# A squared-ReLU MLP by seven products: the fifth and the sixth product of a block trade places

## The chip, the core and the metric

The program runs on one core of one Trainium2 chip. The metric is the device time of one execution, in microseconds (us). Times of an instruction are given in us from the start of the profiled execution's span, or in ns where marked. In the profile PE is the matrix engine (PEld its weight loads), DVE the vector engine, ACT the scalar engine, POOL the GpSimd engine and SP the engine that issues most DMAs.

## The reference

A decoder trunk of two layers on a sequence of 1024 rows and a width of 1024, in float32. Layer 0 mixes tokens with a gated convolution, layer 1 with an attention that has forget gates; each layer then attends to 256 memory tokens and ends in an MLP. The change is in the MLP, which both layers have:

```
def sqrelu_mlp(h, w1, w2):
    return jnp.square(jax.nn.relu(h @ w1)) @ w2        # w1 1024 x 4096, w2 4096 x 1024

h = rmsnorm(x, norm_ff_g[l])
x = x + sqrelu_mlp(h, ff_w1[l], ff_w2[l])
```

## The kernel before

Activations are kept transposed, as 16 tiles of 128 x 512 (`X`, eight chunks of features by two halves of the sequence). Every number that enters a matmul is split into a high part (a rounded float32, made by ACT) and a low part (the rest, made by DVE), and each product of two blocks takes three passes: low by high, high by low, high by high.

**Seven products.** A product of 2 x 2 blocks is made by seven block products instead of eight (Winograd's form). `mlp` writes it as a list, `steps`. One step is one block product for one group `g` of output columns: 4 chunks by 3 passes, 12 matmuls of 128 x 128 by 128 x 512, all into one bank of PSUM. The seven are named after their activation operand, `a11`, `a12`, `a22` (blocks) and `s1` to `s4` (sums of blocks); `WEIGHT` names the partner, and `SUM` tells which of three PSUM sums of the group a product is added to: sum 0 takes `a11`, `a12`; sum 1 takes `s2`, `s3`, `a22`; sum 2 takes `s1`, `s4`. Groups go in pairs, so that a block of the list is 14 steps: the seven products, each for `g` and then for `g + 1`. A pair has six banks (`banks(6)`), and the next pair takes them over in the same order.

**What is read between products.** A sum is read out more than once, because a partial sum is a result too: after `s2` and before `s3` is added, after `s3` and before `a22`, after `s1` and before `s4`, after `a11` and before `a12`. The matmuls of a product therefore wait until the engine that reads the partial sum of its bank has done so: ACT for `a11` (line 805 in the first half, line 955 in the second), DVE for the others (lines 812 and 814 in the first half, 967 and 971 in the second).

**Two halves.** In the first half (h @ w1, groups 0 to 15) the readouts go to `rows`, then `squares` (relu and square, ACT), and the pieces are stored to HBM: `a11` and `a12` split into high and low (`high_inner` on ACT into `uh`, `low_inner` on DVE into `ul`, four tiles in rotation), the sums `s1` to `s4` made of them by POOL (`inner_sums`) and stored by `store_rest`. In the second half (times w2, groups 16 to 31, four groups for each quarter `f` of the inner columns) `load_inner` brings these back, `high_of_inner` and `low_of_inner` split them, and `add_rows` adds the readouts to `X`. For quarter 0 `add_rows` writes into tiles of `X` that had held pieces of the first half, so it also waits for their stores. Groups 0 and 1 are made by eight plain products. The list of the pair 14, 15 (the last of the first half) is ordered by `SEVEN_TURN`, all others by `SEVEN`.

**What sets the order.** Under `in_order` each engine runs its instructions exactly as written. For every step n, `urgent[n]` (the readouts), then `before[n]` (loads, splits, sums) are emitted, then the high part of the weight of step n + 5 and the low part of that of step n + 4, then the 12 matmuls, then `after[n]`. So the readout of a step stands on DVE ahead of a weight's low part that is needed four steps later. DMAs are issued by SP in the same order. With `b` the first step of a block, the code gives positions as `b + 11`; this text counts positions 0 to 13 inside a block.

```
for n in range(len(steps) + 1):
    for f in chain(urgent[n], before[n]):
        f()
    for m, done, f in ((n + AHEAD + 1, highs, fetch_high), (n + AHEAD, fetched, fetch_low)):
        ...
```

Of the kernel before, what the change touches and what calls it, by code (L numbers as in the profile page):

```python
# [41 lines left out]

SEVEN = ("a11", "a12", "s2", "s1", "s4", "s3", "a22")

SEVEN_TURN = ("a11", "a12", "s2", "s3", "s1", "a22", "s4")

ENDING_FIRST = ("a11", "a12", "s2", "s1")
WEIGHT = {"a11": "b11", "a12": "b21", "s2": "t2", "s3": "t3", "s1": "t1", "a22": "t4", "s4": "b22"}  # L50
# [36 lines left out]
def trunk(ctx, tc, a, out):  # L87
# [512 lines left out]
    def mlp(layer, firsts_r, seconds, copy=None, ending=None):  # L600
# [5 lines left out]
        UP = FF // 256  # L606

        ud = {
            x: dram.tile([P, 2, UP, HALF] if x in SPLIT_FIRST else [P, UP, HALF], F32, name=f"u{x}{layer}")
            for x in SEVEN  # L610
        }
# [5 lines left out]
        with (  # L617
# [56 lines left out]
            base = {}  # L674
            for g in range(2, 2 * UP, 2):
                base[g] = len(steps)
                for x in SEVEN if g + 2 != UP else SEVEN_TURN:
                    steps += [(g + i, WEIGHT[x], x, (g + i, SUM[x]), pm) for i in range(2)]
            end = base[2 * UP - 2] + 14
            fetches = [n for n in range(len(steps)) if n not in again]  # L680
# [2 lines left out]
            def at(n, f, *args):  # L683
                before[n].append(partial(f, *args))

            def at_once(n, f, *args):
                urgent[n].append(partial(f, *args))

            def at_end(n, f, *args):
                after[n].append(partial(f, *args))  # L690
# [77 lines left out]
            for g, b in base.items():  # L768
                late = g == UP
# [80 lines left out]
            def split_inner_at(n, g, x):  # L850
                at(n, high_inner, g, x)
                at(n + 1, low_inner, g, x)
# [43 lines left out]
            for g, b in base.items():  # L896
                if g >= UP:
                    continue
                last = g + 2 == UP
                for i in range(2):  # L900
                    for n in range(b + i, b + 14, 2):
                        at_once(n + 1, rows, n)
                        at_end(n + 1, squares, n)
                    if g > 2:
                        split_inner_at(b + 5 + i, g + i, "a11")
                    split_inner_at(b + (14 if last else 11) + i, g + i, "a12")
                    if not last:
                        at(b + 15 + i, inner_sums, g + i, NEW, pool)
                        at(b + 17 + 2 * i, store_rest, g + i)
                    else:  # L910
                        at(b + 13 + i, inner_sums, g + i, NEW[:2], dve)
                        at(b + 15 + i, inner_sums, g + i, NEW[2:], dve)
                        at(b + 16 + i, store_rest, g + i)
# [61 lines left out]
            for f in range(4):  # L975
                lb = base[UP + 4 * f - 2]
                for k, x in enumerate(SEVEN if f else SEVEN_TURN):
                    at(lb + 2 * k + 2, load_inner, f, x)
                late = f == 0
                for x, ns in (  # L980
                    ("s2", (10, 12) if late else (8, 10)), ("s1", (14, 15) if late else (12, 13)), ("s4", (17, 18) if late else (16, 17)),
                    ("s3", (20, 21) if late else (19, 20)), ("a22", (22, 23)),
                ):
                    for j, n in enumerate(ns):
                        at(lb + n, high_of_inner, f, x, j)
                        at(lb + n + 1, low_of_inner, f, x, j)
            b = base[UP]
            for n in range(b, len(steps)):
                g, x = steps[n][0], steps[n][2]
                if x == "a11":  # L990
                    at_once(n + 1, copy_first, g % 4, n)
                    if g >= UP + 4:
                        at(n + 1, add_first, g % 4)
                else:

                    at_once(n + (4 if x in ("a12", "s2") and g < UP + 2 else 1), add_rows, n)
            for i in range(2 * NCH):
                at(b + 30 + 3 * i, load_back, i // 2, i % 2)
                at(b + 32 + 3 * i, add_back, i // 2, i % 2)
# [19 lines left out]
            b = end - 14  # L1019
# [17 lines left out]
            with in_order():  # L1037
# [17 lines left out]
                for n in range(len(steps) + 1):  # L1055
# [5 lines left out]
                    if n < len(steps):  # L1061
                        g, _, x, key, p = steps[n]
# [356 lines left out]
    xd = dram.tile([P, NCH, S], F32, name="xd")  # L1419
    first_normalized, first_weights = [], []  # L1420
    firsts, seconds = mlp(0, *sums, copy=xd, ending=lambda rb: start_fox(rb, first_normalized, first_weights))
    fox_layer(xd, first_normalized, first_weights, seconds)
    firsts, seconds = mlp(1, *mem_attention(1))
    for sl in HALVES:
        rb = firsts if sl.start == 0 else spread(rms_of_sums(seconds, RMS_EPS))
# [73 lines left out]
```

## Time and profile before

| | |
|---|---|
| time, median of 3 runs | 2811.76 us (2811.71 to 2813.89) |
| the profiled execution: its time, its span | 2810.81 us, 2809.0 us |
| PE busy | 2725.0 us, 97% of the span |
| DVE, ACT, POOL busy | 71%, 45%, 26% of the span |
| MLP of layer 0, first to last of its products | 714.8 to 1343.3 us |
| MLP of layer 1 | 2158.0 to 2792.9 us |
| granted clock of PE, mean | 0.993 |

A row of the profile's groups reads: line of the kernel, engine, operation, what it writes and reads, shapes, count | busy us, mean ns of one | idle time of that engine just before such instructions, and who ended most of it. A row of the timeline reads: start, length, engine, line, operation, count, and in brackets the idle time before it and what ended that. PE's matmuls overlap, so that the length of a row and not the mean of one matmul tells the pace.

### The profile page before, as it was taken

To read this page: it belongs to the slowest core of one execution; us is meant where nothing else is said; L and a number is where in the kernel's file an instruction comes from. 1 tells how busy PE (TensorE), PEld (TensorE's weight loads), DVE (VectorE), ACT (ScalarE), POOL (GpSimd) and SP (SyncE) were. 2 spreads that over 40 slices of the span, in tenths; PEclk is the share of its full clock that TensorE was granted. 3 is DMA by queue.
4 is the path that set the end of the run, shared out by engine and by line. 5 is a ranking of instruction groups with operands and counts; after the bars stand their busy time and mean duration, and the time that the engine had idled before them with its cause. 6 is when DMAs were issued, how large, how long until landed. Compare 5 with 4: busy or idle time off the path is not lost. (4 is left out here: it accounts for less than half of the span.)

```text
span 2809.0 us, 35852 instructions
## 1 busy us (share of the span) xinstructions
PE 2725.0 (97%) x12832; PEld 2247.6 (80%) x12832; DVE 1991.7 (71%) x3119; ACT 1275.7 (45%) x2295; POOL 720.2 (26%) x487
## 2 busy tenths in 40 slices
PE   7999999999999999999899999989999999999998
PEld 6777777888888877888688888878888788878886
DVE  5999984555776577777777777775546855677776
ACT  5112143433465563334466666663424655543332
POOL 0000000000076625784000000000000365625763
PEclk9999999999999999999899999999999999999999
DMA  6334364321265585652123222244213455565651
GB/s 220 120 120 135 110 213 124 102 91 56 80 220 181 188 303 195 214 199 91 61 87 94 89 88 77 86 143 138 96 67 105 144 183 191 203 228 194 228 203 60
DMA packets 172275, 402.26 MB, mean 143 GB/s; under 512 B 18352, under 2 KB 47408, under 8 KB 171840
## 3 DMA queue, kind: packets, MB, share of 16 engines
q1 hardware_dynamic: 171840, 399.90, 42.1%
q8 instruction: 101, 1.65, 0.2%
q14 instruction: 78, 0.64, 0.1%
q10 hardware_dynamic: 256, 0.07, 0.0%
HBM read 278.66 MB, written 117.05 MB: 141 GB/s over the span
## 5 line engine op out<-in xcount | busy, mean ns | idle before, releaser
L1070 PE MATMUL mm<-op,w 128*128 128x512 f32 x5424 | 1239.6, 390 | 20.8 <-DVE x L967 8.9
L1070 PEld LDWEIGHTS mm<-op,w 128*128 128x128 f32 x5424 | 1018.5, 188 | 238.7 <-issue 8.9
L269 PE MATMUL mm<-op,wh 128*128 128x512 f32 x1056 | 331.3, 395 | 4.7 <-DVE op L148 4.7
L148 DVE TENSOR_TENSOR w<-r,w 128x512 fp32r<-128x512 f32 x264 | 262.5, 998 | 30.2 <-ACT w L653 30.2
L653 ACT CAST w<-r 128x512 fp32r<-128x512 f32 x264 | 163.4, 623 | 259.9 <-PE mm L1070 235.2
L269 PEld LDWEIGHTS mm<-op,wh 128*128 128x128 f32 x1056 | 200.3, 190 | 50.1 <-DVE op L148 7.9
L1316 PE MATMUL mm<-op,wh 128*128 128x512 f32 x736 | 231.4, 395 | 0.0
L148 DVE TENSOR_TENSOR w<-t,w 128x512 fp32r<-128x512 f32 x180 | 176.6, 995 | 62.3 <-ACT w L653 62.0
L269 PE MATMUL mm<-op,wl 128*128 128x512 f32 x528 | 211.2, 401 | 9.4 <-DVE wl L148 6.2
L647 POOL TENSOR_TENSOR t<-r,t 128x512 f32<-128x512 f32 x104 | 174.1, 1674 | 94.4 <-DVE w L148 63.8
L207 POOL TENSOR_TENSOR r<-v,mhalf 128x4 f32<-128x4 f32 (+1 forms) x15 | 16.8, 1117 | 680.3 <-DVE v L205 680.3
L653 ACT CAST w<-t 128x512 fp32r<-128x512 f32 x180 | 111.9, 622 | 170.6 <-PE mm L1070 140.5
L865 POOL TENSOR_TENSOR x<-x,x 128x512 f32<-128x512 f32 x112 | 160.0, 1453 | 112.5 <-ACT x L878 101.6
L151 ACT CAST wh<-raw 128x1024 fp32r<-128x1024 f32 x96 | 100.6, 1049 | 190.1 <-PE mm L269 102.2
L151 ACT CAST pth<-mm 128x512 fp32r<-128x512 f32 (+1 forms) x224 | 105.9, 496 | 153.5 <-PE mm L556 80.9
L967 DVE TENSOR_TENSOR x<-mm,x 128x512 f32<-128x512 f32 x160 | 109.4, 684 | 93.1 <-PE mm L1070 75.9
L1316 PEld LDWEIGHTS mm<-op,wh 128*128 128x128 f32 x736 | 139.3, 189 | 26.9
L269 PE MATMUL mm<-op,xsh 128*128 128x512 f32 x512 | 158.0, 393 | 0.0
L1316 PE MATMUL mm<-op,wl 128*128 128x512 f32 x368 | 155.5, 423 | 2.4 <-ACT q L1336 2.4
L408 DVE SCALAR_TENSOR_TENSOR x<-d,par,x 128x512 f32<-128x512 f32 x232 | 154.5, 743 | 0.0
L647 POOL TENSOR_TENSOR t<-r,r 128x512 f32<-128x512 f32 x52 | 80.3, 1544 | 288.1 <-DMA r<-in_ff_w 239.2
L148 DVE TENSOR_TENSOR wl<-raw,wh 128x1024 fp32r<-128x1024 f32 x96 | 116.7, 1221 | 37.9 <-ACT wh L151 37.3
(187 smaller groups left out, 4569.2 us busy)
## 6 DMA issues: line engine op xcount, KB each, us to landing
r<-in_ff_w SPq DMA_DIRECT2D x128, 512.0 KB, 3.9
op<-ua SPq DMA_DIRECT2D x80, 512.0 KB, 6.8
us<-x SPq DMA_DIRECT2D x128, 256.0 KB, 2.9
op<-us SPq DMA_DIRECT2D x64, 512.0 KB, 5.3
raw<-mvo SPq DMA_DIRECT2D x32, 512.0 KB, 3.3
ua<-ul SPq DMA_DIRECT2D x64, 256.0 KB, 2.2
ua<-uh SPq DMA_DIRECT2D x60, 256.0 KB, 2.3
raw<-in_pw SPq DMA_DIRECT2D x24, 512.0 KB, 4.6
```

Of the source, the lines that this page charges most:

```text
L148: dve.tensor_tensor(lo, src, hi.bitcast(F32), op=ALU.subtract)
L151: act.copy(hi, src)
L207: pool.tensor_tensor(r, v, mhalf[:, :nb], op=ALU.pow)
L269: pe.matmul(out_ps, x, y, start=i == 0, stop=i == len(terms) - 1)
L408: dve.scalar_tensor_tensor(out[s], d[:, j : j + n], w, y, op0=ALU.mult, op1=ALU.add)
L647: (dve if g in (2, 3, UP, UP + 1) else pool).tensor_tensor(t, raws[g, x], raws[g, y], op=ALU.subtract)
L653: act.copy(highs[n][0], raws[steps[n][:2]])
L865: eng.tensor_tensor(u[g, x], y1, y2, op=op_)
L967: dve.tensor_tensor(v, sums[key], v, op=ALU.add)
L1070: pe.matmul(sums[key], y, z, start=first and i == 0, stop=n == last_of[key] and i == len(terms) - 1, skip_group_check=True,)
L1316: pe.matmul(t, x, y, start=n == 0, stop=n == len(terms) - 1)
```

## The change

The list `SEVEN` gets `s3` ahead of `s4`. It holds for the pairs 2 to 12 of the first half and 16 to 28 of the second. The pair 14, 15 keeps `SEVEN_TURN`, and the last pair, 30, keeps the old order under a new name, `SEVEN_LAST`. Four things follow the swap: the split of `a12` goes from positions 11 and 12 to 13 and 14, because its last piece is added by `s4`; the loads of the second half's operands for quarters 1 to 3 (`for k, x in enumerate(SEVEN ...)`) and the splits of `s3` and `s4` trade their slots; and in quarter 0's first pair the readout of `s2` stands one step earlier, since `s3` now follows it after two steps of `s1`.

```
-SEVEN = ("a11", "a12", "s2", "s1", "s4", "s3", "a22")
+SEVEN = ("a11", "a12", "s2", "s1", "s3", "s4", "a22")
 SEVEN_TURN = ("a11", "a12", "s2", "s3", "s1", "a22", "s4")
+SEVEN_LAST = ("a11", "a12", "s2", "s1", "s4", "s3", "a22")
...
-                for x in SEVEN if g + 2 != UP else SEVEN_TURN:
+                for x in {UP - 2: SEVEN_TURN, UP: SEVEN, 2 * UP - 2: SEVEN_LAST}.get(g, SEVEN):
...
-                    split_inner_at(b + (14 if last else 11) + i, g + i, "a12")
+                    split_inner_at(b + (14 if last else 13) + i, g + i, "a12")
...
-                    ("s2", (10, 12) if late else (8, 10)), ("s1", (14, 15) if late else (12, 13)), ("s4", (17, 18) if late else (16, 17)),
-                    ("s3", (20, 21) if late else (19, 20)), ("a22", (22, 23)),
+                    ("s2", (10, 12) if late else (8, 10)), ("s1", (14, 15) if late else (12, 13)), ("s3", (17, 18) if late else (16, 17)),
+                    ("s4", (20, 21) if late else (19, 20)), ("a22", (22, 23)),
...
-                    at_once(n + (4 if x in ("a12", "s2") and g < UP + 2 else 1), add_rows, n)
+                    at_once(n + (({"a12": 4, "s2": 3}.get(x, 1)) if g < UP + 2 else 1), add_rows, n)
```

The order on PE at positions 8 to 11 of pair 16, 17 in the MLP of layer 1. The number behind `mm_` is the bank's name: 20577 and 20594 are sum 1 of groups 16 and 17, 20612 and 20632 (20633 in the changed kernel) are sum 2. Before:

```order
L1070 MATMUL mm_20612<-op_20468,w_20557 128x512 x6
L1070 MATMUL mm_20612<-op_20469,w_20557 128x512 x6
L1070 MATMUL mm_20632<-op_20468,w_20574 128x512 x6
L1070 MATMUL mm_20632<-op_20469,w_20574 128x512 x6
L1070 MATMUL mm_20577<-op_20325,w_20591 128x512 x6
L1070 MATMUL mm_20577<-op_20326,w_20591 128x512 x6
L1070 MATMUL mm_20594<-op_20325,w_20609 128x512 x6
L1070 MATMUL mm_20594<-op_20326,w_20609 128x512 x6
```

And in the changed kernel:

```order
L1071 MATMUL mm_20577<-op_20325,w_20557 128x512 x6
L1071 MATMUL mm_20577<-op_20326,w_20557 128x512 x6
L1071 MATMUL mm_20594<-op_20325,w_20574 128x512 x6
L1071 MATMUL mm_20594<-op_20326,w_20574 128x512 x6
L1071 MATMUL mm_20612<-op_20468,w_20591 128x512 x6
L1071 MATMUL mm_20612<-op_20469,w_20591 128x512 x6
L1071 MATMUL mm_20633<-op_20468,w_20609 128x512 x6
L1071 MATMUL mm_20633<-op_20469,w_20609 128x512 x6
```

`s3` (sum 1, operands 20325 and 20326) moved ahead of `s4` (sum 2, operands 20468 and 20469); `a22` follows into 20577 and 20594 in both. Between two products into one bank stand three steps instead of one, except for `a11` and `a12`.

The order on DVE at the same place, from the readouts of `s2` and `s1` on (line 971 and, in the changed kernel, 972; lines 967 and 968 are the later readouts, 148 and 149 the low parts of operands `op` and weights `w`). Before:

```order
L971 TENSOR_TENSOR x41_15721<-mm_20612,m_20491 128x512
L148 TENSOR_TENSOR op_20325<-op_20325 128x1024
L148 TENSOR_TENSOR w_20609<-r11_17856,w_20609 128x512
L971 TENSOR_TENSOR x40_15720<-mm_20577,m_20491 128x512
L971 TENSOR_TENSOR x51_15723<-mm_20632,m_20523 128x512
L148 TENSOR_TENSOR op_20326<-op_20326 128x1024
L148 TENSOR_TENSOR w_20629<-t_20462,w_20629 128x512
L971 TENSOR_TENSOR x50_15722<-mm_20594,m_20523 128x512
L967 TENSOR_TENSOR x40_15720<-mm_20612,x40_15720 128x512
L148 TENSOR_TENSOR op_20413<-op_20413 128x1024
L148 TENSOR_TENSOR w_20650<-t_20494,w_20650 128x512
L967 TENSOR_TENSOR x50_15722<-mm_20632,x50_15722 128x512
```

And in the changed kernel:

```order
L972 TENSOR_TENSOR x40_15720<-mm_20577,m_20491 128x512
L972 TENSOR_TENSOR x41_15721<-mm_20612,m_20491 128x512
L149 TENSOR_TENSOR op_20468<-op_20468 128x1024
L149 TENSOR_TENSOR w_20609<-r11_17856,w_20609 128x512
L972 TENSOR_TENSOR x50_15722<-mm_20594,m_20523 128x512
L972 TENSOR_TENSOR x51_15723<-mm_20633,m_20523 128x512
L149 TENSOR_TENSOR op_20469<-op_20469 128x1024
L149 TENSOR_TENSOR w_20630<-t_20462,w_20630 128x512
L968 TENSOR_TENSOR x41_15721<-mm_20577,x41_15721 128x512
L149 TENSOR_TENSOR op_20413<-op_20413 128x1024
L149 TENSOR_TENSOR w_20651<-t_20494,w_20651 128x512
L968 TENSOR_TENSOR x51_15723<-mm_20594,x51_15723 128x512
```

The readout of `s2` (20577 and 20594 into `x40` and `x50`) moved up by one step, and the readouts of `s3` took the place of those of `s4`. The number and the kinds of instructions are the same.

The order on ACT where pair 2, 3 of layer 1 ends and pair 4, 5 begins (lines 796 and 797, in the changed kernel 797 and 798, are relu and square; 839 or 840 is the high part of `a12`; 805 or 806 the readout of `a11`; 653 or 654 the high part of a weight). Before:

```order
L839 CAST uh_18549<-x70_15726 128x512
L653 CAST w_18552<-r00_17853 128x512
L796 ACTIVATE x20_15716<-x20_15716 128x512
L797 ACTIVATE x20_15716<-x20_15716 128x512
L839 CAST uh_18573<-x00_15712 128x512
L653 CAST w_18576<-r10_17855 128x512
L796 ACTIVATE x60_15724<-x60_15724 128x512
L797 ACTIVATE x60_15724<-x60_15724 128x512
L653 CAST w_18599<-t_18522 128x512
L796 ACTIVATE x10_15714<-x10_15714 128x512
L797 ACTIVATE x10_15714<-x10_15714 128x512
L653 CAST w_18619<-t_18526 128x512
```

And in the changed kernel, up to the readout of `a11`:

```order
L840 CAST uh_18587<-x70_15726 128x512
L654 CAST w_18590<-t_18522 128x512
L797 ACTIVATE x10_15714<-x10_15714 128x512
L798 ACTIVATE x10_15714<-x10_15714 128x512
L840 CAST uh_18613<-x00_15712 128x512
L654 CAST w_18616<-t_18526 128x512
L797 ACTIVATE x21_15717<-x21_15717 128x512
L798 ACTIVATE x21_15717<-x21_15717 128x512
L806 COPY x01_15713<-mm_18619 128x512
```

The two casts of `a12` moved down by two steps and now stand between the squares of `a22` and right ahead of the readout of the next pair's `a11`.

## The prediction, made before the changed kernel ran

> **What bounds the kernel now.** I read the page's busy shares, then its groups of matmuls, then PE's timeline through both MLPs.
>
> ```profile
> PE 2725.0 (97%) x12832; PEld 2247.6 (80%) x12832; DVE 1991.7 (71%) x3119; ACT 1275.7 (45%) x2295; POOL 720.2 (26%) x487
> L1070 PE MATMUL mm<-op,w 128*128 128x512 f32 x5424 | 1239.6, 390 | 20.8 <-DVE x L967 8.9
> ```
>
> PE is the bound, and the matmuls of the two MLPs (line 1070) fill 1239.6 us of it. The idle time ahead of them is 20.8 us in all, so an order of these products can give back little more than that. The timeline shows each wait with its place: a row is an unbroken run of matmuls, with the idle time ahead of it in brackets. Layer 0, then layer 1:
>
> ```profile
> 793.53 239.65 PE L1070 MATMUL mm<-op,w 128*128 128x512 f32 x1056 [0.39 <-DVE x L814]
> 1036.40 27.54 PE L1070 MATMUL mm<-op,w 128*128 128x512 f32 x120 [3.22 <-ACT m L955]
> 1066.14 65.55 PE L1070 MATMUL mm<-op,w 128*128 128x512 f32 x288 [2.20 <-DVE x L967]
> 1131.89 11.21 PE L1070 MATMUL mm<-op,w 128*128 128x512 f32 x48 [0.20 <-DVE x L967]
> 1143.72 65.53 PE L1070 MATMUL mm<-op,w 128*128 128x512 f32 x288 [0.62 <-DVE x L967]
> 1209.76 11.17 PE L1070 MATMUL mm<-op,w 128*128 128x512 f32 x48 [0.51 <-DVE x L967]
> 1221.25 111.82 PE L1070 MATMUL mm<-op,w 128*128 128x512 f32 x492 [0.32 <-DVE x L967]
> ```
>
> ```profile
> 2165.33 71.00 PE L1070 MATMUL mm<-op,w 128*128 128x512 f32 x312
> 2239.49 241.28 PE L1070 MATMUL mm<-op,w 128*128 128x512 f32 x1056 [3.16 <-DVE x L814]
> 2483.09 27.51 PE L1070 MATMUL mm<-op,w 128*128 128x512 f32 x120 [2.33 <-ACT m L955]
> 2513.18 77.94 PE L1070 MATMUL mm<-op,w 128*128 128x512 f32 x336 [2.58 <-DVE x L967]
> 2592.13 65.55 PE L1070 MATMUL mm<-op,w 128*128 128x512 f32 x288 [1.01 <-DVE x L967]
> 2658.32 11.19 PE L1070 MATMUL mm<-op,w 128*128 128x512 f32 x48 [0.64 <-DVE x L967]
> 2669.81 76.57 PE L1070 MATMUL mm<-op,w 128*128 128x512 f32 x336 [0.31 <-DVE x L967]
> 2746.94 35.64 PE L1070 MATMUL mm<-op,w 128*128 128x512 f32 x156 [0.55 <-DVE x L967]
> ```
>
> Twelve matmuls are a step, so the counts give each wait its position in the list. The twelve waits for a DVE readout (lines 814 and 967) all stand at position 8, ahead of `s4`, or at position 12, ahead of `a22`: the runs of 48 matmuls, four steps, go from the one to the other. Both are products that follow, with only one step between, a product into their own bank. The two waits for ACT (line 955) stand at position 2 of pair 16, where `a12` follows `a11` at the same distance; the change leaves that distance as it is. Of the pairs in the first half only the first (groups 2, 3) waits at all; five pairs then run through in the 1056 matmuls.
>
> One step takes (239.65 - 65.55) / ((1056 - 288) / 12) = 2.720 us. A run is longer than its steps by 65.55 - 24 x 2.720 = 0.27 us, which is lost once at each wait, beside the idle time.
>
> **What the change removes.** Idle ahead of the twelve: 0.39 + 2.20 + 0.20 + 0.62 + 0.51 + 0.32 = 4.24 us in layer 0, and 3.16 + 2.58 + 1.01 + 0.64 + 0.31 + 0.55 = 8.25 us in layer 1. The ends of twelve runs: 12 x 0.27 = 3.2 us. And the clock, in stretches right after three of the waits (third number from the end):
>
> ```profile
> 1036.40:1039.40 3.00, 3.00 (x13) 2.46 (x14) 3.00 (x6) 3.00 (x6) 0.00 (x0) 1.00 0.54 183
> 2239.40:2242.40 3.00, 2.91 (x8) 2.30 (x9) 3.00 (x5) 2.95 (x6) 3.00 (x3) 0.58 0.30 112
> 2513.00:2515.60 2.60, 2.42 (x6) 1.97 (x7) 2.31 (x4) 0.00 (x0) 0.56 (x1) 0.50 0.00 0
> ```
>
> After the two waits in layer 1 PE was granted 0.58 and 0.50 of its clock. The price stands in the timeline: the same 1056 matmuls took 241.28 us there and 239.65 in layer 0, the same 336 took 77.94 and later 76.57. That is 1.63 + 1.37 = 3.0 us. Sum: 4.24 + 8.25 + 3.2 + 3.0 = **18.7 us** hang on the waits that the change addresses.
>
> The Trainium skill, TensorE: Matmul & The Clock Gate (HAM oscillation), lets the clock fall only when PE idles for more than a window of some 3.4 us. The trace disagrees: half clock after 2.58 and 3.16 us, full clock after 3.22. By that rule the 3.0 us would have another cause and stay, and the sum would be 15.7 us.
>
> **Does the readout come in time?** The change makes no engine do less; it gives DVE two more steps, 5.4 us, for each readout. A wait goes if DVE is less late than that and nothing else it owes comes too late instead. In the second half it is latest in pair 16 of layer 1; DVE there:
>
> ```profile
> 2497.04 0.69 DVE L971 TENSOR_TENSOR x<-mm,m 128x512 f32<-128x512 f32 x1 [0.88 <-PE mm L1070]
> ...
> 2500.59 2.21 DVE L148 TENSOR_TENSOR op<-op 128x1024 fp32r<-128x1024 f32 x1
> 2502.72 1.78 DVE L148 TENSOR_TENSOR w<-t,w 128x512 fp32r<-128x512 f32 x1
> 2504.42 0.68 DVE L971 TENSOR_TENSOR x<-mm,m 128x512 f32<-128x512 f32 x1
> 2505.03 0.67 DVE L967 TENSOR_TENSOR x<-mm,x 128x512 f32<-128x512 f32 x1
> ...
> 2509.05 1.71 DVE L148 TENSOR_TENSOR op<-op 128x1024 fp32r<-128x1024 f32 x1
> 2512.36 0.68 DVE L967 TENSOR_TENSOR x<-mm,x 128x512 f32<-128x512 f32 x1
> ```
>
> At 2497.04 DVE is on time, since it waited for PE. Then low parts of 1.7 to 2.2 us each put it behind, and the readout of `s3` that `a22` waits for ends at 2513.04. PE was ready at 2483.09 + 10 x 2.720 = 2510.3. In the new order the readout of `s2` at 2504.42 has gone one step up, the other one of `s2` likewise (into the idle 0.88 us), and the readout of `s3` has the slot of `s4`'s, the row at 2505.03, now without a readout right ahead of it. It ends at about 2505.1 and PE is ready at 2510.3, with 5 us in hand. What else `a22` needs: the low part of its second operand tile, 2509.05 to 2510.76 in both orders or somewhat earlier, is used from the seventh matmul on, at 2510.3 + 1.4 = 2511.7; 0.9 us in hand, the tightest of all. The weights' low parts are made four steps ahead. Then the first pair of layer 1, DVE:
>
> ```profile
> 2231.42 0.68 DVE L814 TENSOR_TENSOR x<-mm,x 128x512 f32<-128x512 f32 x1
> ...
> 2235.39 0.68 DVE L814 TENSOR_TENSOR x<-mm,x 128x512 f32<-128x512 f32 x1
> ...
> 2238.76 0.68 DVE L814 TENSOR_TENSOR x<-mm,x 128x512 f32<-128x512 f32 x1
> ...
> 2244.13 0.69 DVE L814 TENSOR_TENSOR x<-mm,x 128x512 f32<-128x512 f32 x1 [0.22 <-PE mm L1070]
> ```
>
> The first two are the readouts of `s4`, the third that of `s3`, for which PE waited from 2165.33 + 26 x 2.720 = 2236.1. `s3` takes the first slot, done at 2232.1, and for group 3 the second, done at 2236.1 and needed one step after 2236.1. At 2244.13 DVE waits for PE again: the lateness is a bout of some 5 us, which the new distance covers. The other eight waits are of 0.2 to 1.0 us, and 5.4 us cover them.
>
> **What it adds and moves.** The readout of `s2` in pair 16, one step earlier, writes tiles of `X` whose stores must have landed. SP's last stores there, and their time to landing:
>
> ```profile
> 2492.38 2.01 SPq L826 DMA_DIRECT2D us<-x  x3
> DMA to landing us min/median/max: 4.1/4.5/5.7
> ```
>
> The last is issued by 2494.4 and lands by 2498.9, at the worst by 2500.1. The later of the two readouts stands behind low parts until 2499.4 or so, and PE needs it at position 9, 2483.09 + 7 x 2.720 = 2502.1: nothing, and up to 0.7 us of DVE's time at the worst. The loads of `s3` and `s4` trade slots of one kind and size: nothing, covered by more than four steps between load and use. The additional waits in PE's program (one for the readout, one for the low part, where one stood for both) cost nothing, as steps with either take 2.720 us. The split of `a12` is the one piece that moves towards something: it now stands on ACT right ahead of the readout of the next pair's `a11`, for which `a12` waits after one step. ACT at such a place, the start of pair 6 of layer 1, and in all waits of the trace those of that cast (us in total, times, longest):
>
> ```profile
> 2287.68 0.59 ACT L805 COPY x<-mm 128x512 f32<-128x512 f32 x1 [0.70 <-PE mm L1070]
> ACT uh L839 <- DMA ua<-uh: 13.4, 7, 3.8
> ```
>
> ACT idled 0.70 us for PE's sum there, and a cast takes 0.6. The readout ends at 2287.68 + 0.59 = 2288.27; PE needs it when the one step between is done, at about 2287.68 + 2.72 = 2290.4, less some 0.2 us from a sum's end to the readout's start. So 1.9 us more are in hand: nothing, unless the cast itself waits.
>
> **The rivals.**
>
> - *Part of it stays* (chance 0.20). Pair 16 gets a wait at position 8 or 9 for `s2`, or the low part of `a22` comes 0.9 us later, so that 2.20 + 2.58 + 2 x 0.27 + 1.37 = 6.7 us remain; or layer 0's 4.24 + 6 x 0.27 = 5.9 us vanish in the attention's start behind it, if that hangs on a DMA. Gain 12 to 13 us: 2799 to 2800. For it: the small margin of 0.9 us. Against it: all other margins.
> - *Nothing is gained* (0.12). DVE is 71% busy and does the same work; if its lateness only grew until the next thing it owes, PE would wait there: 2811. Against it: the idle time at 2244.13.
> - *Slower* (0.06). The casts of `a12` wait for their `uh` tile, as they did 7 times for 13.4 us, now ahead of `a11`'s readout. Six pairs in each layer have them; with a wait of 3.8 us at each, less the 0.70 and 1.9 us in hand and plus 0.6 for the second cast, PE loses 1.8 us twelve times and, at half clock after each, 1.4 more: 38 us against 18.7, 2831. It decides from 1.6 us of lost time at each. Against it: the tile is free two steps later than before, and the waits lie in the first pair.
> - *The clock's part stays* (0.05): 15.7 us gained, 2796, if the half clock does not come from these waits; the two rows at 0.58 and 0.50, each right after one of them, speak against it. It is what the rule of the Trainium skill above would have.
>
> **How the numbers follow.** The profiled execution took 2810.81 us (span 2809.0); the median of the runs is 0.95 us above it. 2811.76 - 18.7 = 2793.1, so I forecast **2793 us** (chance 0.57), 2790 to 2797 for this case alone: 3 us up if the two waits that stay (3.22 and 2.33 us) now fall so that half clock follows them, 3 us down if they shrink. With the first rival and a little beyond both ends the range is **2789 to 2804 us**. A measurement of this kernel can tell about 0.2%, 5.6 us, from no change: faster by more than that 0.82 (the forecast, the first and the last rival), the same 0.12, slower 0.06.
>
> **What would show it.** Right: no run of matmuls broken at positions 8 and 12, runs from position 2 of pair 16 to the end of an MLP over 100 steps long, idle time ahead of the matmuls near 8 us instead of 20.8, full clock in both MLPs. Wrong: waits on line 972 ahead of `s3` in pair 16; waits on weights' or operands' low parts ahead of `a22`; waits on ACT's line 806 ahead of `a12` in the first half.

## The result and the profile after

The changed kernel takes 2799.22 us, the median of 6 runs (2798.00 to 2801.56). The kernel before, run beside it, takes 2812.82 us (6 runs, 2809.71 to 2815.79). The ratio is 0.995 with a 95% interval of 0.9938 to 0.9962: faster by 13.6 us, where 18.7 were forecast. The profiled executions stand 11.6 us apart, 2810.81 and 2799.19 us (spans of 2809.0 and 2797.4).

In the changed kernel all lines are one further down: the matmuls are line 1071, ACT's copy of `a11` 956, DVE's readouts 968 and 972. The page's busy shares and its group of these matmuls:

```profile
PE 2723.1 (97%) x12832; PEld 2249.7 (80%) x12832; DVE 2013.5 (72%) x3119; ACT 1275.7 (46%) x2295; POOL 729.3 (26%) x487
L1071 PE MATMUL mm<-op,w 128*128 128x512 f32 x5424 | 1237.6, 390 | 12.8 <-ACT m L956 9.7
```

PE's timeline through the two MLPs, with the idle time ahead of each unbroken run in brackets:

```profile
779.77 251.31 PE L1071 MATMUL mm<-op,w 128*128 128x512 f32 x1108
1035.52 292.94 PE L1071 MATMUL mm<-op,w 128*128 128x512 f32 x1284 [4.45 <-ACT m L956]
...
2160.94 81.88 PE L1071 MATMUL mm<-op,w 128*128 128x512 f32 x360
2243.12 228.77 PE L1071 MATMUL mm<-op,w 128*128 128x512 f32 x1008 [0.30 <-ACT x L806]
2477.14 294.09 PE L1071 MATMUL mm<-op,w 128*128 128x512 f32 x1284 [5.25 <-ACT m L956]
```

The twelve waits at positions 8 and 12 are gone. From position 2 of pair 16 on, each layer runs 1284 matmuls, 107 steps, without a break. But the idle time ahead of these matmuls fell from 20.8 to 12.8 us only, since the two waits that were to stay have grown, from 3.22 to 4.45 us and from 2.33 to 5.25, and half clock now follows both. The clock is the third number from the end:

```profile
1035.50:1038.50 3.00, 2.98 (x8) 0.54 0.49 169
2477.10:2480.10 3.00, 2.96 (x7) 0.50 0.51 149
2480.10:2483.10 3.00, 3.00 (x8) 0.52 0.96 335
```

Call the place where pair 14 gives way to pair 16 *the turn*. By the starts of its steps, what positions 1 to 3 of pair 16 take beyond three steps of 2.72 us is 3.55 us in layer 0 and 2.64 in layer 1 before, and 6.35 and 8.30 after: 8.5 us more, of which 4.2 are idle time and the rest half clock. From the first step of an MLP to its last, layer 0 got 3.1 us shorter (625.63 to 622.52) and layer 1 6.9 (631.96 to 625.03).

What stands behind the wait, on ACT and on DVE, in layer 1 of the changed kernel:

```profile
2474.80 0.62 ACT L654 CAST w<-t 128x512 fp32r<-128x512 f32 x1 [2.74 <-DVE t L648]
2475.33 0.63 ACT L797 ACTIVATE x<-x 128x512 f32<-128x512 f32 x1
2475.98 0.63 ACT L798 ACTIVATE x<-x 128x512 f32<-128x512 f32 x1
2476.52 0.57 ACT L956 COPY m<-mm 128x512 f32<-128x512 f32 x1
```

```profile
2466.50 0.69 DVE L648 TENSOR_TENSOR t<-r,r 128x512 f32<-128x512 f32 x1 [2.88 <-DMA r<-in_ff_w]
2467.23 0.69 DVE L648 TENSOR_TENSOR t<-r,t 128x512 f32<-128x512 f32 x1
...
2472.70 0.68 DVE L648 TENSOR_TENSOR r<-r 128x512 f32<-128x512 f32 x1
2473.30 0.68 DVE L648 TENSOR_TENSOR t<-r,r 128x512 f32<-128x512 f32 x1
2474.02 1.29 DVE L648 TENSOR_TENSOR t<-r,t 128x512 f32<-128x512 f32 x2
```

`a12` waits for ACT's copy of `a11`'s sum. The copy stands in ACT's queue behind a weight's cast (line 654), and that cast stood 2.74 us for a difference `t` that DVE makes (line 648). DVE in turn had stood 2.88 us for a raw weight load, and then worked without a gap until the `t` was ready. Four raw loads serve a pair, two for each group; the two that matter below are the second one of group 16 (called r01, after its tile) and the second one of group 17 (r11), which lands some 3.8 us after r01. The copies for group 16 and group 17 are line 956 in order.

### The profile page after: what moved, and what is told of

Read it like the earlier page. It is cut to its first block, busy times and chain, and to the rows that moved or that the text cites. A ratio compares the mean times of both kernels' runs of the same rounds, so it can differ in the third digit from the quotient of the medians.

```text
span 2797.4 us, 35830 instructions
## 1 busy us (share of the span) xinstructions
PE 2723.1 (97%) x12832; PEld 2249.7 (80%) x12832; DVE 2013.5 (72%) x3119; ACT 1275.7 (46%) x2295; POOL 729.3 (26%) x487
## 5 line engine op out<-in xcount | busy, mean ns | idle before, releaser
L1071 PE MATMUL mm<-op,w 128*128 128x512 f32 x5424 | 1237.6, 390 | 12.8 <-ACT m L956 9.7
L149 DVE TENSOR_TENSOR w<-r,w 128x512 fp32r<-128x512 f32 x264 | 274.4, 1043 | 32.8 <-ACT w L654 20.9
L149 DVE TENSOR_TENSOR w<-t,w 128x512 fp32r<-128x512 f32 x180 | 198.8, 1119 | 32.9 <-ACT w L654 32.9
L866 POOL TENSOR_TENSOR x<-x,x 128x512 f32<-128x512 f32 x112 | 165.6, 1502 | 112.5 <-ACT x L879 101.6
```

Source lines behind the costliest of these rows:

```text
L149: dve.tensor_tensor(lo, src, hi.bitcast(F32), op=ALU.subtract)
L866: eng.tensor_tensor(u[g, x], y1, y2, op=op_)
L1071: pe.matmul(sums[key], y, z, start=first and i == 0, stop=n == last_of[key] and i == len(terms) - 1, skip_group_check=True,)
```

## The experiments

Each was timed beside the kernel before, whose median was 2812.03 us beside the first four, 2815.09 beside the next four, 2812.09 beside the two after them and 2814.09 beside the last two. A ratio is that of the kernel to the kernel before, with its 95% interval.

The first theory, *the stores*: splitting `a12` also stores it, two groups by a high and a low part, four DMAs of 256 KB on SP. The change puts those of pair 12 two steps later, right ahead of the loads of the turn, so that these land later. The rival: nothing is to be had there, PE merely waits off what it gained before.

### Pair 12 in the old order, its stores where they were

```
-for x in {UP - 2: SEVEN_TURN, ...
+for x in {UP - 4: SEVEN_LAST, UP - 2: SEVEN_TURN, ...
-    split_inner_at(b + (14 if last else 13) + i, g + i, "a12")
+    split_inner_at(b + (14 if last else 11 if g == UP - 4 else 13) + i, g + i, "a12")
```

> The changed kernel, but pair 12, 13 (the last but one of the first half) keeps the old order and its a12 split at positions 11 and 12. Theory 'stores': the wait for ACT at position 2 of pair 16 grew (3.22 to 4.45 us in layer 0, 2.33 to 5.25 in layer 1, each with half clock behind it) because the four stores of pair 12's a12 now go out two steps later, into the stretch where SP's loads for pair 16 queue; then the two waits return to about 3.2 and 2.3 us at full clock, and the time is some 8 us under the changed kernel's 2799, about 2791. Rival 'nothing to gain there': the loads at the turn end when they end, and whatever PE wins ahead of it is waited off at position 2; then the waits stay at 4.4 and 5.2 us and the time at 2799.

Measured: 2793.94 us (2791.34 to 2801.73, 5 runs), ratio 0.9937 (0.9915 to 0.9960), some 5 us better than the changed kernel by the medians, though the runs of the two overlap. The wait at position 2 is 3.40 us in layer 0, near what the stores theory has (but at 0.67 of the clock over the next 3 us, not at full clock), and 4.67 in layer 1, nearer to the rival. One trace does not decide; the profiled execution was the slowest of the five.

### Only the split of pair 12 moved, in the kernel before

```
-    split_inner_at(b + (14 if last else 11) + i, g + i, "a12")
+    split_inner_at(b + (14 if last else 13 if g == UP - 4 else 11) + i, g + i, "a12")
```

> The kernel before, with one thing moved: the a12 split of pair 12, 13 at positions 13 and 14 instead of 11 and 12; the order of products is the old one. 'Stores': the waits at position 2 of pair 16 grow by 1 to 3 us each and half clock follows, 2812 + 8 = 2820. 'Nothing to gain there': PE wins nothing ahead of the turn, so the waits stay at 3.2 and 2.3 us and the time at 2812.

Measured: 2816.53 us (2813.93 to 2820.56, 10 runs), ratio 1.0019 (1.0006 to 1.0033): slower by 4.5 us (1.7 to 9.3 by the interval), with nothing of the change but this move. PE's timeline at the turn of the two layers (here and below, the last row of a view ends where the view ends):

```profile
1036.67 21.66 PE L1070 MATMUL mm<-op,w 128*128 128x512 f32 x84 [5.28 <-ACT m L955]
...
2487.45 12.75 PE L1070 MATMUL mm<-op,w 128*128 128x512 f32 x45 [4.29 <-ACT m L955]
```

Both waits are 2 us longer than before (3.22 and 2.33). In layer 0 PE gained nothing ahead of the wait: pair 14 begins 274.70 us after the MLP's first step, and 274.69 before. There the stores do it, and the rival cannot explain it. In layer 1 this trace does not decide: pair 14 begins 276.54 us after the first step instead of 279.08, since the wait in pair 2 was shorter here (2.23 us, and full clock after it), so that the rival would have a longer wait at the turn too.

### The split of pair 12 one step later instead of two

```
-    split_inner_at(b + (14 if last else 13) + i, g + i, "a12")
+    split_inner_at(b + (14 if last else 12 if g == UP - 4 else 13) + i, g + i, "a12")
```

> The changed kernel with the a12 split of pair 12, 13 one step earlier (positions 12 and 13). 'Stores': the growth of the waits at position 2 of pair 16 shrinks by about half, to some 3.8 us in both layers, 2795. 'Nothing to gain there': 4.4 and 5.2 us as in the changed kernel, 2799.

Measured: 2799.62 us (2794.51 to 2799.89, 5 runs), ratio 0.9950 (0.9933 to 0.9967); waits of 3.47 and 4.68 us, with 0.72 and 0.50 of the clock over the 3 us behind them. In layer 0 the wait lies between those of the change (4.45 us) and of the first experiment (3.40), in layer 1 it is that of the first experiment. The time does not tell: three of the five runs stand at the changed kernel's 2799 to 2800 us, two at 2794.5.

### The swap in the second half alone

```
-for x in {UP - 2: SEVEN_TURN, UP: SEVEN, 2 * UP - 2: SEVEN_LAST}.get(g, SEVEN):
+for x in {UP - 2: SEVEN_TURN, 2 * UP - 2: SEVEN_LAST}.get(g, SEVEN_LAST if g < UP else SEVEN):
-    split_inner_at(b + (14 if last else 13) + i, g + i, "a12")
+    split_inner_at(b + (14 if last else 11) + i, g + i, "a12")
```

> The swap in the second half alone; the first half keeps the old order and the old place of the a12 split. Both theories: the ten waits of the second half vanish, the two of pair 2 stay (3.16 + 0.39 idle, 2 x 0.27, 1.63 for the clock = 5.7 us), the waits at position 2 of pair 16 stay as before; 18.7 - 5.7 = 13 us under before, 2799. If the ten are not worth 13 us, the term of the sum was wrong.

Measured: 2799.00 us (2790.10 to 2805.23, 6 runs), ratio 0.9950 (0.9930 to 0.9971): 13.0 us below the kernel before, as much as the whole change brings. The ten waits of the second half are gone, the first half's two stay (1.52 and 2.92 us), and the waits at the turn are 3.58 and 2.77. The turn costs 5.5 and 3.1 us at its positions 1 to 3 here, 6 us less in all than in the changed kernel (6.35 and 8.30). The two MLPs together take 1247.4 us here and 1247.6 in the changed kernel. So the first half's part of the change wins two waits and pays for them at the turn.

### Which landing decides

Over the six traces of before, the change and these four kernels (twelve turns), the landing of r11 minus the time lost at the step ahead of position 2 is 36.70 us each time, counted from the first step of pair 14. The page's chain of waits names r11 too. In the changed kernel:

```profile
2453.95 7.41 DMA op<-us
2461.42 8.90 DMA r<-in_ff_w
2470.37 1.22 DVE op L149
```

So the theory became: r11 lands late, and ACT's order passes it on to the copy. Two edits act on these two factors.

**The copies ahead of the late cast.** ACT copies the sums of positions 0 and 1 ahead of the squares, and the late cast is issued a step later.

```
-at_once(n + 1, copy_first, g % 4, n)
+(after[n].insert if g < UP + 2 else urgent[n + 1].insert)(
+    0 if g < UP + 2 else 99, partial(copy_first, g % 4, n))
-for m, done, f in ((n + AHEAD + 1, highs, fetch_high), ...
+for m, done, f in ((n + AHEAD + (n not in (base[UP], base[UP] + 1)), highs, fetch_high), ...
```

> The changed kernel; at the turn to the second half (pair 16) ScalarE copies the first sums of positions 0 and 1 ahead of the squares, and the weight cast that waits for the last raw load (the weights of position 5) is issued one step later, behind the first copy. Nothing else differs. The theory (ScalarE's order: TensorE stands at position 2 because the copy is queued behind a cast that waits for the load) expects the wait at position 2 to fall from 4.45 and 5.25 us to under 1 us, a wait of 0.5 to 1.3 us at position 3 (the second copy still stands behind the cast), no half clock ahead of position 4, and of the 14.6 us that positions 1 to 3 cost over their steps some 10 to come back: 2787 to 2791 us. The rival (the load itself is late: whoever is spared the queue waits for the weights at position 5) expects 3 us or more of waiting to turn up at positions 4 and 5 on VectorE's low parts, and 2794 us or more.

Measured: 2791.97 us (2789.87 to 2799.12, 5 runs), ratio 0.9935 (0.9911 to 0.9959): 23.1 us below the kernel before. Two of the five runs stand at 2799 us, above the 2787 to 2791 expected. PE's timeline at the turn of layer 1, and ACT's:

```profile
2470.01 3.04 PE L1071 MATMUL mm<-op,w 128*128 128x512 f32 x12 [0.20 <-ACT m L956]
2474.23 8.45 PE L1071 MATMUL mm<-op,w 128*128 128x512 f32 x36 [1.19 <-ACT m L956]
```

```profile
2469.38 0.57 ACT L956 COPY m<-mm 128x512 f32<-128x512 f32 x1
...
2473.08 0.61 ACT L654 CAST w<-t 128x512 fp32r<-128x512 f32 x1
2473.60 0.58 ACT L956 COPY m<-mm 128x512 f32<-128x512 f32 x1
```

The wait at position 2 is gone in both layers (0.20 us is left in layer 1), a second one of 1.19 us (0.95 in layer 0) stands at position 3, where the second copy is still behind the cast. No wait takes its place at positions 4 and 5, and at position 6 there is one of 0.3 us in each layer, where the rival expected 3 us or more. That the copy hung in ACT's queue is shown.

**r11 earlier.** It goes ahead of the two loads of `s1`'s operand in SP's queue; nothing else moves.

```
-at(b - 6 + i + 2 * late, load_raw, g + i, 1)
+at(b - 6 + i + late, load_raw, g + i, 1)
```

> The changed kernel; the two second raw loads of pair 16 are issued one step earlier, so that the last of them stands ahead of the two loads of the operand s1 in SyncE's queue. ScalarE's order is that of the changed kernel. The theory that the landing of this load decides (the wait was the landing minus 36.7 us in all twelve cases) expects it to land two transfers or 2.5 us earlier, the wait at position 2 to be 2.0 us in the first layer and 2.8 in the second, most of the half clock gone, and 2789 to 2792 us. The rival (the transfers end when they end, some other one is then waited for) expects the same wait on another load and 2797 to 2800 us.

Measured: 2799.80 us (2797.23 to 2802.74, 10 runs), ratio 0.9948 (0.9936 to 0.9960), the changed kernel's. The trace has r11 at 39.88 and 38.79 us after the first step of pair 14, in layer 1 3.3 us earlier than in the changed kernel, and the waits are 5.59 and 4.49 us:

```profile
2461.64 1.19 SPq L640 DMA_DIRECT2D r<-in_ff_w  x2
...
2469.41 0.69 DVE L648 TENSOR_TENSOR t<-r,r 128x512 f32<-128x512 f32 x1 [2.90 <-DMA r<-in_ff_w]
...
2480.05 10.29 PE L1071 MATMUL mm<-op,w 128*128 128x512 f32 x34 [4.49 <-ACT m L956]
```

The theory of r11 fell. What the edit did not move in the queue is r01: DVE still stands 2.90 us for it, and from there to PE's start it is 2480.05 - 2469.41 = 10.64 us, as in the changed kernel (2477.14 - 2466.50 = 10.64). In the six kernels above r11 only came a fixed 3.84 us behind it.

**Both edits together.**

> The changed kernel with both edits: the copies first and the last raw load ahead of s1's. If the queue order and the landing are the two factors of one wait, the wait at positions 2 and 3 together is under 1.5 us in each layer, and the time is 2785 to 2789 us. If the rival holds (late weights move the wait to positions 4 and 5) the gain over either edit alone is under 1 us.

Measured: 2791.11 us (2790.31 to 2791.44, 4 runs), ratio 0.9922 (0.9897 to 0.9946): within 1 us of the copies alone, as it must be if r11 does not count, and above the 2785 to 2789 expected. The rival had that size, but not for its reason: positions 4 and 5 have no wait, and position 6 one of 0.3 us.

**Both, and pair 12 as in the first experiment.**

> Both edits on the kernel whose pair 12 keeps the old order with its splits of a12 two steps earlier (it took 2793.94 us). If the turn no longer hangs on when the loads land, the earlier stores bring nothing more, and the time is that of both edits on the changed kernel within 2 us (2785 to 2789). If the landing still decides, it is 2 to 4 us faster than that one.

Measured: 2788.00 us (2785.94 to 2789.44, 4 runs), ratio 0.9910 (0.9885 to 0.9936), 3 us below the one without pair 12's old order, and the runs of the two do not overlap. The landing still counts: r01 comes at 36.18 and 35.47 us instead of 37.06 and 37.83, and what is lost at positions 1 to 3 falls from 1.3 and 2.1 us to 0.4 and nothing.

**r01 earlier.** The mirror of the edit of r11: now r01 goes ahead of two operand loads, those of `s3`, and r11 stays.

```
-at(lb + 2 * k + 2, load_inner, f, x)
+at(lb + 2 * k + (4 if not f and x == "s3" else 2), load_inner, f, x)
```

> The changed kernel; of SyncE's queue one place is different: the second raw load of group 16 goes ahead of the two loads of the operand s3 instead of behind them. The second raw load of group 17 stays where it was. In the fourteen turns traced with ScalarE's order unchanged, the extra time ahead of position 2 was the landing of group 16's load minus 32.85 us, also where group 17's load was put two transfers earlier. The theory that this landing decides (VectorE stands for it, and its eight us of work behind it, with the difference that ScalarE's cast needs, end that much later) expects the load 2.5 us earlier, the wait at position 2 down from 4.45 and 5.25 us to 1.9 to 2.9 us, and 2789 to 2793 us. The rival (the first load of the operand s2, for which ScalarE stands 4 to 5 us at that time, decides, and the raw load only follows it in the queue at a fixed distance) expects the same waits as in the changed kernel and 2797 to 2800 us.

Measured: 2792.78 us (2790.01 to 2795.99, 4 runs), ratio 0.9938 (0.9919 to 0.9956): 19.3 us below the kernel before. SP, DVE and PE in layer 1, and PE in layer 0:

```profile
2452.92 0.54 SPq L640 DMA_DIRECT2D r<-in_ff_w  x1
2453.55 2.95 SPq L937 DMA_DIRECT2D op<-us  x4
2457.49 0.33 SPq L640 DMA_DIRECT2D r<-in_ff_w  x1
```

```profile
2459.98 0.69 DVE L648 TENSOR_TENSOR t<-r,r 128x512 f32<-128x512 f32 x1 [0.49 <-DMA r<-in_ff_w]
```

```profile
1031.29 3.93 PE L1071 MATMUL mm<-op,w 128*128 128x512 f32 x11 [1.95 <-ACT m L956]
...
2470.62 4.64 PE L1071 MATMUL mm<-op,w 128*128 128x512 f32 x19 [2.90 <-ACT m L956]
```

The waits fell from 4.45 and 5.25 us to 1.95 and 2.90, while r11 landed no earlier than in the changed kernel. The first load of `s2` did not either (31.2 and 31.9 us after the first step of pair 14, and 31.1 and 31.9 in the changed kernel), so that rival fell. And again 2470.62 - 2459.98 = 10.64 us lie between DVE's start and PE's. Landings of r01 and r11 in us after the first step of pair 14, and the time lost at the step ahead of position 2, in layer 0 / layer 1 (from the traces, ACT's order unchanged):

| kernel | r01 | r11 | lost | r01 less lost | r11 less lost |
|---|---|---|---|---|---|
| before | 36.24 / 35.35 | 40.08 / 39.20 | 3.38 / 2.49 | 32.86 / 32.86 | 36.70 / 36.70 |
| swap in second half alone | 36.59 / 35.78 | 40.44 / 39.62 | 3.74 / 2.93 | 32.86 / 32.85 | 36.70 / 36.69 |
| split moved, old order | 38.30 / 37.31 | 42.14 / 41.15 | 5.44 / 4.45 | 32.86 / 32.86 | 36.70 / 36.70 |
| pair 12 old | 36.41 / 37.69 | 40.25 / 41.52 | 3.56 / 4.83 | 32.86 / 32.85 | 36.70 / 36.69 |
| split one step later | 36.49 / 37.70 | 40.32 / 41.54 | 3.63 / 4.85 | 32.85 / 32.86 | 36.69 / 36.69 |
| the change | 37.46 / 38.26 | 41.30 / 42.10 | 4.61 / 5.41 | 32.86 / 32.85 | 36.70 / 36.69 |
| r11 earlier | 38.61 / 37.52 | 39.88 / 38.79 | 5.75 / 4.66 | 32.86 / 32.86 | 34.13 / 34.13 |
| r01 earlier | 34.97 / 35.92 | 41.38 / 42.32 | 2.11 / 3.07 | 32.86 / 32.86 | 39.27 / 39.25 |

r01 explains all sixteen turns to 0.01 us. The same traces settle the first experiment. SP's queue in layer 1, from the last of pair 12's stores (`ua<-uh`, `ua<-ul`) to the first operand loads of the turn (`op<-ua`), before and after:

```profile
2436.67 0.32 SPq L845 DMA_DIRECT2D ua<-ul  x1
2437.08 3.61 SPq L639 DMA_DIRECT2D r<-in_ff_w  x2
2441.36 2.15 SPq L934 DMA_DIRECT2D op<-ua  x4
```

```profile
2430.17 2.25 SPq L640 DMA_DIRECT2D r<-in_ff_w  x2
2432.83 0.33 SPq L846 DMA_DIRECT2D ua<-uh  x1
2433.26 0.37 SPq L846 DMA_DIRECT2D ua<-ul  x1
2433.73 2.77 SPq L935 DMA_DIRECT2D op<-ua  x4
```

Pair 14 begins at 2437.09 us before and at 2428.21 after, so the last store is issued 0.4 us ahead of it before and 5.1 us behind it after, past the raw loads, and the operand loads start at 4.3 and 5.5 us. Among the first six kernels of the table the first operand load has landed at 9.7 to 10.4 us where the stores are early, at 11.5 to 11.9 where they come two steps later, and at 9.9 and 11.9 with one step. Behind it the transfers run back to back. In the changed kernel (the last two numbers are the DMA share and GB/s):

```profile
2443.00:2453.00 10.00, 10.00 (x46) 8.29 (x45) 6.81 (x11) 2.13 (x5) 1.07 (x1) 1.00 1.03 401
2453.00:2463.00 10.00, 10.00 (x46) 8.28 (x45) 4.98 (x8) 4.64 (x8) 0.00 (x0) 1.00 1.04 396
```

From the first landing to r01's the same transfers took 24.95 to 27.56 us over the first six kernels of the table. Layer 1 with pair 12 in the old order had the longest of these (first landing at 10.1 us, r01 27.56 later), so its 4.67 us of waiting were a slow stretch and not the stores. The rival, that PE waits off in layer 1 what it gained ahead, does not hold there: with both edits and pair 12 in the old order, pair 14 of layer 1 begins 274.0 us after the MLP's first step, 5.1 us earlier than before, and r01 lands 35.47 us after that beginning, as it did before (35.35). The stores are worth 1.5 to 2 us in each layer, and the stretch scatters by as much.

**r01 earlier and the copies ahead.**

> The changed kernel with that load earlier and with the two copies ahead of the squares and of the late cast. The theory expects no wait over 0.5 us at positions 2 and 3 in either layer, and 2784 to 2789 us, though pair 12's stores stay two steps later. The rival expects no more than the copies alone gave: 2790 to 2793 us.

Measured: 2786.92 us (2783.48 to 2787.51, 4 runs), ratio 0.9910 (0.9895 to 0.9926): 25.2 us below the kernel before and the lowest median of all, though not apart from the 2788.00 above, with pair 12's stores as late as in the changed kernel. The page's group of the MLPs' matmuls, and PE's timeline in layer 1:

```profile
L1071 PE MATMUL mm<-op,w 128*128 128x512 f32 x5424 | 1233.2, 389 | 3.0 <-DVE w L149 2.8
```

```profile
2153.28 339.45 PE L1071 MATMUL mm<-op,w 128*128 128x512 f32 x1495
2492.91 262.56 PE L1071 MATMUL mm<-op,w 128*128 128x512 f32 x1157 [0.18 <-DVE op L149]
```

Nothing is left of the turn's waits at positions 2 and 3, in either layer. The 0.18 us are at position 12 of pair 16, for the low part of the second operand tile of `a22`.

### What the change is worth without the turn

The two edits, once on the kernel before and once on the changed kernel, on one chip.

> The kernel before, with the two edits at the turn (group 16's second raw load ahead of s3's loads, the two copies ahead of the late cast) and nothing of the change. The theory (the change is worth the 18.7 us of the forecast, and the turn took 9 of them back) expects no wait at position 2 of pair 16, the twelve waits at positions 8 and 12 as before, a gain over the kernel before of what its turn cost there, 6.2 us (2805 to 2808), and 18 to 20 us more than the changed kernel with the same edits. The rival (the forecast's sum was too large by itself) expects 10 to 14 us between the two.

> The changed kernel with the same two edits, the second of the two to be compared (it took 2786.92 us in the run before). Theory: 2785 to 2789 us, 18 to 20 us below the kernel before with these edits. Rival: 10 to 14 us below it.

Measured: 2801.63 us (2800.65 to 2805.35, 5 runs) with the old order and 2789.52 (2788.23 to 2790.24, 4 runs) with the new: ratios of 0.9961 (0.9948 to 0.9975) and 0.9915 (0.9897 to 0.9933). The two stand 12.1 us apart by the medians, 15.1 by the profiled executions (2805.35 and 2790.24), and 14.1 by the two MLPs in these (1248.44 and 1234.38 us, first step to last); the profiled execution of the old order was the slowest of its five. The 18 to 20 us of the theory fell, and the medians lie in the rival's 10 to 14. The edits alone gave 12.5 us and not the 6.2 that the theory had for them (9.15 of them in the MLPs of the traces). In the old order with the edits, the group of matmuls, then PE's timeline at the second half of layer 0 and at the largest waits of layer 1:

```profile
L1070 PE MATMUL mm<-op,w 128*128 128x512 f32 x5424 | 1238.1, 390 | 13.2 <-DVE x L967 6.8 <-DVE x L814 3.5 <-DVE w L148 2.8
```

```profile
1060.55 76.42 PE L1070 MATMUL mm<-op,w 128*128 128x512 f32 x336 [1.61 <-DVE x L967]
1137.15 65.56 PE L1070 MATMUL mm<-op,w 128*128 128x512 f32 x288 [0.18 <-DVE x L967]
...
2238.33 268.51 PE L1070 MATMUL mm<-op,w 128*128 128x512 f32 x1176 [3.06 <-DVE x L814]
2508.45 76.57 PE L1070 MATMUL mm<-op,w 128*128 128x512 f32 x336 [1.60 <-DVE x L967]
```

The waits at position 12 of pair 16 are now 1.61 and 1.60 us instead of 2.20 and 2.58, and after the second one the same 336 matmuls take 76.57 us, full clock, instead of 77.94. So some 3 of the 18.7 us went with the waits at the turn, ten steps ahead; that DVE's lateness carries them from there is likely, but no run shows it. Without the turn the twelve waits cost 15.2 us (6.8 + 3.5 = 10.3 idle, 3.2 at run ends, 268.51 - 98 x 2.720 - 0.27 = 1.7 of clock), and of these the change brings 14.1 in the traces and 12.1 by the medians. Part of what is missing is new, small waits in layer 0 of the changed kernel with the edits:

```profile
1032.58 26.36 PE L1071 MATMUL mm<-op,w 128*128 128x512 f32 x115 [0.17 <-ACT m L956]
1059.46 262.56 PE L1071 MATMUL mm<-op,w 128*128 128x512 f32 x1157 [0.52 <-DVE op L149]
```

The 0.52 us are again ahead of the low part that `a22` needs at position 12, the one for which the prediction had 0.9 us in hand. In all five changed kernels with the copies ahead PE stood 0.18 to 0.52 us for it, in one layer each.

## Why the prediction was right and wrong

**The sum of what is removed: right as an account of the old trace, too large as the worth of the change alone.** All twelve waits went, and with them the run ends and the half clock behind two of them. No readout came too late: no wait on line 968 or 972 anywhere, no wait for a low part ahead of `a22`. In the profiled execution 18.7 us less 8.5 at the turn and 0.6 in pair 4 makes 9.6; the two MLPs together are 10.0 us shorter. The other 1.4 us between the executions lie ahead of the first MLP, which the change does not touch. But some 3 of the 18.7 us were there only with the turn's waits in the old order: without these the same change is worth 12 us by the medians and 14 in the MLPs of the traces.

**The two waits at position 2 of pair 16: wrong, and the step that failed.** The prediction took them as fixed, "the change leaves that distance as it is", with 3 us up or down for the clock. It looked at the order of the products and not at what the wait hangs on: the landing of r01, through DVE's work and ACT's queue, 10.64 us to the matmul in every trace with ACT's order unchanged. It had quoted both rows of ACT's line 955 without following them back.

**The split of `a12`: "nothing", wrong by its DMAs.** The prediction costed the casts on ACT, and there it was nearly right: of the twelve places where the split now stands ahead of a readout one shows a wait, 0.30 us (0.6 with the run's end). It left out the four stores that the split also issues. Those of pair 12 now stand at the front of the stretch in which the DMA engines are full, and put its first landing 1.7 us back in layer 0 (10.14 to 11.88) and 1.5 in layer 1 (10.40 to 11.86). That is more than the growth of the wait in layer 0 (1.2 us) and half of it in layer 1 (2.9); there the other half is the stretch itself, which took longer, and by the scatter of the traces that may be chance. By itself the move cost 4.5 us (1.7 to 9.3), as the second experiment shows.

**The clock.** The 3.0 us behind the two waits of layer 1 came back, so they did come from the waits, and the rival by which the clock's part stays fell. What was forecast as 3 us up at the turn happened, for a wait that grew and not for one that stayed: half clock follows both waits now, in layer 1 the step at position 2 itself takes 5.29 us instead of 2.72, and over both layers the lost clock there is about half of the 8.5 us.

**The rivals.** The time, 2799.2 us, is the one of "part of it stays" (2799 to 2800), but not by its mechanism: pair 16 has no wait at position 8 or 9, and from layer 0's MLP to layer 1's it is 0.2 us longer, not 6. "Slower" is there in small, in pair 4 of layer 1, at 0.6 us instead of 38. "Nothing is gained" fell. None of them had a transfer at the turn. So that the time lies inside the stated 2789 to 2804 us is in part luck: the case that was forecast ended at 2797, and the part of the range above it was there for waits that did not come. Of the signs of being right, the unbroken runs came true; idle time near 8 us and full clock in both MLPs did not.

## What to carry to other kernels

When a step is moved, list its DMAs with its instructions, and look at what the queue carries at the new place: 1 MB stored two steps later cost more than the moved casts, because the loads that follow it run back to back, and one of them is waited for. A wait that the change "leaves as it is" is not a constant; follow it back to what lands last, across each queue that passes it on, before taking it as one. And what a chain of waits names as last need not be what decides: an edit that moves only that one transfer tells, and the same edit on its neighbour tells which of the two it is.

## What the runs showed of the hardware

**Half clock does not follow from the length of the idle time alone.** Over the first 3 us behind PE's wait at position 2 it was granted the full clock after waits of 2.33, 2.77, 2.90 and 3.22 us, 0.73 of it after 1.95, 0.67 to 0.73 after the three of 3.40 to 3.58, and 0.50 to 0.54 after the eight of 4.29 us and more. The two of the kernel with r01 earlier, layer 0 (1.95 us) and layer 1 (2.90 us), the clock third from the end:

```profile
1031.30:1034.30 3.00, 3.00 (x10) 2.41 (x11) 3.00 (x6) 3.00 (x6) 0.00 (x0) 0.73 0.51 173
2470.70:2473.70 3.00, 3.00 (x13) 2.46 (x14) 3.00 (x7) 3.00 (x6) 0.00 (x0) 1.00 0.43 143
```

The Trainium skill, TensorE: Matmul & The Clock Gate (HAM oscillation), sets the bound at idle gaps of about 3.4 us. For all eleven waits from 3.40 us on the traces agree; the 1.95 us here, and the 2.58 and 3.16 us of the kernel before, are below it and lost clock too.

**The same run of loads takes longer or shorter by up to 2.6 us**, 24.95 to 27.56 us for the same transfers in one queue, at some 400 GB/s (401 and 396 in the two rows of the changed kernel above). A wait that hangs on its end moves one to one with it, so that a single trace can't tell an effect of 1 or 2 us there.
